# First MLP of a two-layer trunk: 14 of the 16 pairs of up blocks by a Strassen scheme with seven products

## The chip, the cores and the metric

The kernel runs on one core of a Trainium2 chip, in one launch. The metric is the device time of that launch in microseconds (us); lower is better. Engines are called as the profile calls them: PE is TensorE's matmul, PEld its weight load, DVE is VectorE, ACT is ScalarE, POOL is GpSimd, SP is SyncE, which here issues DMAs.

## The reference

512 tokens of width 1024 pass two layers. Layer 0 mixes by an attention over chosen keys, layer 1 by a gated depthwise convolution; each is followed by an MLP of width 4096 with a squared ReLU. Cut to what matters:

```python
def reference(x, ...):
    h = x                                    # 1 x 512 x 1024, fp32
    for i in range(2):
        hn = rmsnorm(h, norm_mix_g[i])
        h = h + (dsa_mixer if i == 0 else conv_mixer)(hn, ...)
        h = h + sq_relu_mlp(rmsnorm(h, norm_mlp_g[i]), mlp_w1[i], mlp_w2[i])
    return rmsnorm(h, final_g)
# sq_relu_mlp(x, w1, w2) = square(relu(x @ w1)) @ w2, w1 1024 x 4096, w2 4096 x 1024
```

The change touches the MLP of layer 0, and what stands at its two ends.

## The kernel before

Activations lie transposed, 128 features by 512 tokens a tile; `hT[c]` (c = 0 to 7) is the residual. An fp32 product is made of three matmuls with operands of type fp32r: high part by high part, high by low, low by high (`mm3`, L91 to L93). `scaled` makes the two parts of the activations, `ghi[c]` on ACT (L174) and `glo[c]` on DVE (L175). `split` makes those of a piece of weights, 128 rows by 4 x 128: `whi` on ACT (L86), `wlo` on DVE (L87). Such a piece is called a unit here; it feeds 12 matmuls. Weights come in loads of 1 MB (L76, on SP's queue, two buffers `wraw`): one load is two blocks of 128 output columns, four units. Split units wait in the pool `wsplit_mid` (12 buffers of each part).

The MLP runs in four groups of 1024 hidden features. A group has 8 up blocks (`up_proj`: 24 matmuls of 512 columns each into a PSUM bank; then `hr` on DVE, which is ReLU and the norm's scale, `hf` and `hh`, two squares on ACT, and `hl` on DVE, the low part of the square) and 8 down blocks of 24 matmuls (`proj` on the hidden tiles; DVE adds each to `hT[c]`). The norm's factor `rmsb` isn't ready when the first MLP starts, so block 0 runs before it. All engines take their instructions in the order that the tile framework's scheduler wrote down; only the last down projection has PE's order by hand, since there the norm of the next mixer and the first products of its projection (`pw1_first`) are woven in. `stacked_taps` makes the diagonal matrices of the convolution on POOL (33 operations, L700) after group 0.

Of the kernel before, what the change touches and what calls it, by code (L numbers as in the profile page):

```python
# [18 lines left out]
P = 128  # L19
# [21 lines left out]

WHOLE = 5

ROW = 512
FILL = 64


@with_exitstack
def kernel(
# [24 lines left out]
    def load(w, k0, kn, c0, cn):  # L74
        t = wraw.tile([P, kn, cn], F32, tag="wraw", name="wraw")
        nc.sync.dma_start(t, rows(w)[:, k0:k0 + kn, c0:c0 + cn])  # L76
        return t

    wsplit = []

    def split(src, eng=None, pool=None, tag="w", bufs=None):

        a, b = src.shape[1], src.shape[2]
        hi, lo = ((pool or wsplit[-1]).tile([P, whole(a * b)], F32R, tag=tag + x, name=tag + x, bufs=bufs)
                  [:, :a * b].rearrange("p (a b) -> p a b", a=a) for x in ("hi", "lo"))
# [50 lines left out]
        return block  # L136


    fill = small.tile([P, FILL // 4], F32, name="fill")
    nc.gpsimd.memset(fill, 0.0)  # L140
    ident = const.tile([P, P], F32, name="ident")
    make_identity(nc, ident)
    ones = const.tile([P, P], F32, name="ones")
# [73 lines left out]


    w_in = dsa_w_in[0]
    with tc.tile_pool(name="wsplit_att", bufs=5) as ws, \  # L220
            tc.tile_pool(name="att", bufs=1) as att, \
            tc.tile_pool(name="att_ps", bufs=2, space=PSUM) as att_ps:

        wsplit.append(ws)

        def lg():
            return att_ps.tile([P, S], F32, tag="lg", name="lg")
# [398 lines left out]
                    wo_end(c, oproj([c])[0])  # L626


    def up_proj(w, rr, pool, st=None, block=None, ahead=()):

        block = block or proj(w, g2)
        hid = []

        def hidden(ps):
            r = pool.tile([P, S], F32, tag="hr", name="hr", bufs=2)
            nc.vector.scalar_tensor_tensor(r, ps, 0.0, rr[0], op0=OP.max, op1=OP.mult)  # L636
            f = pool.tile([P, S], F32, tag="hf", name="hf", bufs=2)
            nc.scalar.activation(f, r, AF.Square)
            th = pool.tile([P, S], F32R, tag="hh", name="hh", bufs=10)
            tl = pool.tile([P, S], F32R, tag="hl", name="hl", bufs=10)  # L640
            nc.scalar.activation(th, r, AF.Square)  # L641
            nc.vector.tensor_sub(tl, f, th.bitcast(F32))  # L642
            hid.append((th, tl))

        done = 0
        if st is not None:
            first = list(ahead) or block([0])
            cols = rms_cols(st)
            first += block([1]) if len(first) < 2 else []
            rr[:] = [broadcast(cols, NB, bank("bc"))]  # L650
            for ps in first:
                hidden(ps)
            done = 2
        for j in range(done, KC):
            hidden(block([j])[0])
        return hid

# [4 lines left out]
    def pw1_first(k):  # L662

        for i, p in enumerate((aproj, gproj)):
# [7 lines left out]
    conv_ctx = ExitStack()
    late = conv_ctx.enter_context(tc.tile_pool(name="late", bufs=1))
    diags = [late.tile([P, max(TAPS0[c][0], TAPS1.get(c, (0, 0))[0]), 4, 32], F32, name=f"diag{c}")
             for c in range(KC)]

    def stacked_taps(pool):

        cw4 = pool.tile([P, 2 * P], F32, name="cw4")
        sel = pool.tile([P, 32], F32, name="sel")
        nc.gpsimd.tensor_add(sel, ident[:, 0:32], ident[:, 32:64])
        for z in (2, 3):
            nc.gpsimd.tensor_add(sel, sel, ident[:, z * 32:(z + 1) * 32])
        ps = bank("cw4_ps")
        for i in range(2):
            r = pool.tile([P, 4, 32], F32, name=f"cwr{i}")
            if i:
                nc.gpsimd.memset(r, 0.0)  # L690
            for a in range(4 - i):
                t = 16 * i + 4 * a
                nc.sync.dma_start(r[a * 32:(a + 1) * 32],
                                  conv_w_dw[0][t:t + 4].rearrange("s (g i) -> g s i", i=32))
            nc.tensor.transpose(ps[:, i * P:(i + 1) * P], r.rearrange("p s i -> p (s i)"), ident)
        nc.vector.tensor_copy(cw4, ps[:, :2 * P])
        for c in range(KC):
            for a in range(diags[c].shape[1]):
                k0 = a * 32 + 4 * c
                nc.gpsimd.tensor_mul(diags[c][:, a], sel.unsqueeze(1).to_broadcast([P, 4, 32]),  # L700
                                     cw4[:, k0:k0 + 4].unsqueeze(2).to_broadcast([P, 4, 32]))

    with tc.tile_pool(name="mlp", bufs=1) as mlp:
        rr = []
        for g in range(NG - 1):
            hid = up_proj(mlp_w1[0][:, g * D:(g + 1) * D], rr, mlp, st if g == 0 else None)
            down = proj(mlp_w2[0][g * D:(g + 1) * D, :], hid)
            for c in range(KC):
                nc.vector.tensor_add(hT[c], down([c])[0], hT[c])
            if g == 0:  # L710
                stacked_taps(mlp)
        hid = up_proj(mlp_w1[0][:, DFF - D:], rr, mlp)
        down = proj(mlp_w2[0][DFF - D:, :], hid)
        st = rms_start()
        with tc.manual_schedule(engines={PE}):
            for c in range(KC):
                nc.vector.tensor_add(hT[c], down([c])[0], hT[c])
                scaled(c, vec("mix", KC + c))
                rms_add(st, c)
                if c:  # L720
                    pw1_first(c - 1)
            aps = aproj([1], kept=pw1_kept[0], ks=range(4), last=False)
            pw1_first(KC - 1)
            ps = bank("rms_ps")
            cols = rms_cols(st, ps)
            aproj([1], kept=pw1_kept[0], pss=aps, ks=range(4, KC), first=False)
            rr = [broadcast(cols, NB, ps)]
            table(AF.Sigmoid, ghi[KC - 1].bitcast(F32))


    HS = S // 2
    halves = [slice(0, HS), slice(HS, S)]
    with tc.tile_pool(name="cv", bufs=1) as cv, \
            tc.tile_pool(name="dram", bufs=1, space=bass.MemoryType.DRAM) as dram, \
# [6 lines left out]
        with tc.tile_pool(name="cv_t", bufs=2) as cv_t:  # L741
# [14 lines left out]
            def taps(c, cs, npe, npool):  # L756
# [13 lines left out]
                w = n + 4 * (npe - 1)  # L770
                flat = dram.tile([P, w + 3], F32, name=f"flat{c}_{cs.start}")
                nc.sync.dma_start(flat, sh(0, w + 3 - n))
                sh4 = cv_t.tile([P, 4, S + 4 * (TAPS // 4 - 1)], F32, tag="sh4", name="sh4")
                for z in range(4):
                    nc.sync.dma_start(sh4[z * 32:(z + 1) * 32, :, :w],
                                      flat.rearrange("(j i) x -> i j x", j=4)[:, :, z:z + w])
# [166 lines left out]
    with tc.tile_pool(name="m2", bufs=1) as m2, \  # L943
# [95 lines left out]
```

## Time and profile before

| | |
|---|---|
| time, median of 3 runs | 1187.97 us (1187.29 to 1189.49) |
| the profiled execution | 1186.75 us, span 1185.0 us (1.75 us lie around the span) |
| PE, PEld busy | 1150.8 us (97%), 948.5 us (80%) |
| DVE, ACT, POOL busy | 663.3 us (56%), 498.2 us (42%), 247.5 us (21%) |
| the first MLP | about 281 to 645 us |

Busy times of PE overlap, since its matmuls are pipelined, so spacing is read from the starts of successive matmuls. In a row of a timeline the numbers in square brackets are the idle time of the engine ahead of it, and what released it; a row with xN is N instructions without a gap. A window row gives, for a stretch, each engine's busy time with its count, then TensorE's granted clock as a share of full speed, the share of the DMA engines and GB/s.

### The profile page before, as it was taken

What the parts mean: (1) busy time and instruction counts of PE and PEld (TensorE: products, weight loads), DVE (VectorE), ACT (ScalarE), POOL (GpSimd) and SP (SyncE); (2) the same over time, 40 slices, a digit from 0 to 9 for tenths busy, and PEclk for the clock granted to TensorE, in tenths of its full rate; (3) what the DMA queues carried; (4) which work ended last, traced back from release to release, by engine and by line L of the source; (5) the groups of instructions that cost most, each with busy time, mean ns of one, the idle gap of its engine ahead of it and who ended that gap; (6) DMA issues with size and microseconds to landing.
All of it is one profiled execution on the core that took longest, in us unless ns stands there. A gap on an engine that the chain in (4) does not pass through costs nothing.

```text
span 1185.0 us, 15284 instructions
## 1 busy us (share of the span) xinstructions
PE 1150.8 (97%) x5828; PEld 948.5 (80%) x5828; DVE 663.3 (56%) x1195; ACT 498.2 (42%) x936; POOL 247.5 (21%) x248
## 2 busy tenths in 40 slices
PE   7999999999999999999999988899999999999997
PEld 6778888877888888888888666689888888888886
DVE  4589854476434434434444998878544434434434
ACT  5353454545423423423435544466632432432422
POOL 2436643322005000000012667632100000000000
PEclk8999999999999999999999998999999999999999
DMA  6122222215233323322323563533322332332211
GB/s 229 36 71 72 89 84 77 71 36 182 78 100 107 98 80 107 107 83 78 125 71 116 151 172 91 161 108 115 117 86 92 107 107 72 106 107 92 86 36 71
DMA packets 104353, 117.84 MB, mean 99 GB/s; under 512 B 3817, under 2 KB 87609, under 8 KB 104280
## 3 DMA queue, kind: packets, MB, share of 16 engines
q1 hardware_dynamic: 102440, 112.89, 30.6%
q10 hardware_dynamic: 1840, 3.97, 0.9%
q8 instruction: 46, 0.75, 0.3%
q14 instruction: 27, 0.22, 0.1%
HBM read 112.56 MB, written 4.29 MB: 99 GB/s over the span
## 4 chain that ended last, share of the span: by engine, by line
PE 81%; DVE 12%; DMA 2%; issue 2%; ACT 1%; POOL 1%; SPq 0%; POOLq 0%; DVEq 0%; ACTq 0%
PE mm L91 19%; PE mm L93 19%; PE mm L92 19%; PE dps L93 5%; PE dps L92 5%; PE dps L91 5%; DVE score L482 2%; DVE m L480 2%; DVE conv L802 2%; DVE wlo L87 2%; DVE pa L798 1%; PE vps L91 1%; PE vps L92 1%; PE vps L93 1%; DMA xs<-in_x_dram 1%
## 5 line engine op out<-in xcount | busy, mean ns | idle before, releaser
L86 ACT ACTIVATE whi<-wraw 128x512 fp32r<-128x512 f32 x378 | 234.6, 631 | 469.9 <-PE mm L92 317.1
L92 PE MATMUL mm<-glo,whi 128*128 128x512 f32 (+1 forms) x928 | 337.0, 365 | 1.2 <-DVE glo L175 1.2
L93 PE MATMUL mm<-ghi,wlo 128*128 128x512 f32 (+1 forms) x928 | 337.1, 365 | 0.0
L91 PE MATMUL mm<-ghi,whi 128*128 128x512 f32 (+1 forms) x928 | 334.6, 366 | 1.9 <-ACT whi L86 0.8
L87 DVE TENSOR_TENSOR wlo<-wraw,whi 128x512 fp32r<-128x512 f32 x325 | 233.5, 726 | 177.7 <-ACT whi L86 174.1
L92 PEld LDWEIGHTS mm<-glo,whi 128*128 128x128 f32 x928 | 175.0, 189 | 31.0 <-issue 2.4
L91 PEld LDWEIGHTS mm<-ghi,whi 128*128 128x128 f32 x928 | 173.1, 189 | 32.6 <-issue 2.8
L93 PEld LDWEIGHTS mm<-ghi,wlo 128*128 128x128 f32 x928 | 175.0, 189 | 28.7 <-issue 1.1
L93 PE MATMUL mm<-hh,wlo 128*128 128x512 f32 x256 | 99.6, 389 | 0.0
L92 PE MATMUL mm<-hl,whi 128*128 128x512 f32 x256 | 99.6, 389 | 0.0
L92 PE MATMUL dps<-wlo,hh 128*128 128x512 f32 x256 | 99.6, 389 | 0.0
L91 PE MATMUL mm<-hh,whi 128*128 128x512 f32 x256 | 99.1, 389 | 0.0
L91 PE MATMUL dps<-whi,hh 128*128 128x512 f32 x256 | 99.1, 389 | 0.0
L93 PE MATMUL dps<-whi,hl 128*128 128x512 f32 x256 | 98.6, 389 | 0.0
L636 DVE SCALAR_TENSOR_TENSOR hr<-mm,rmsb 128x512 f32<-128x512 f32 x64 | 44.1, 691 | 91.9 <-PE mm L93 90.2
L87 POOL TENSOR_TENSOR wlo<-wraw,whi 128x512 fp32r<-128x512 f32 x53 | 70.9, 1342 | 89.6 <-ACT whi L86 89.5
L183 POOL TENSOR_TENSOR fr<-v,mhalf 128x1 f32<-128x1 f32 x4 | 2.2, 548 | 340.2 <-DVE v L181 340.2
L642 DVE TENSOR_TENSOR hl<-hf,hh 128x512 fp32r<-128x512 f32 x64 | 44.6, 697 | 41.9 <-ACT hh L641 41.9
L206 POOL TENSOR_TENSOR ss<-sq 128x512 f32<-128x512 f32 (+1 forms) x4 | 5.7, 1434 | 270.3 <-ACT sq L201 270.3
L790 POOL TENSOR_TENSOR pa<-pa,pt 128x512 f32<-128x512 f32 (+1 forms) x43 | 53.6, 1249 | 32.6 <-ACT pt L788 30.5
L92 PEld LDWEIGHTS mm<-hl,whi 128*128 128x128 f32 x256 | 48.0, 188 | 10.1
L92 PEld LDWEIGHTS dps<-wlo,hh 128*128 128x128 f32 x256 | 48.0, 188 | 10.0
(257 smaller groups left out, 1588.2 us busy)
## 6 DMA issues: line engine op xcount, KB each, us to landing
wraw<-in_mlp_w_dram SPq DMA_DIRECT2D x64, 1024.0 KB, 5.2
wraw<-in_conv_w_pw_dram SPq DMA_DIRECT2D x12, 1024.0 KB
wraw<-in_dsa_w_in_dram SPq DMA_DIRECT2D x10, 1024.0 KB, 9.1
wraw<-in_dsa_w_out_dram SPq DMA_DIRECT2D x4, 1024.0 KB, 4.9
sh<-flat SPq DMA_DIRECT2D x12, 260.0 KB, 3.6
sh<-flat SPq DMA_DIRECT2D x20, 138.0 KB, 2.8
xw<-in_dsa_w_in_dram ACTq DMA_DIRECT2D x4, 584.0 KB, 7.4
xs<-in_x_dram SPq DMA_DIRECT2D x4, 512.0 KB, 12.1
```

The lines of the kernel that those rows point to most:

```text
L86: nc.scalar.activation(hi, src, AF.Copy)
L87: (eng or nc.vector).tensor_sub(lo, src, hi.bitcast(F32))
L91: nc.tensor.matmul(ps, wh, xh, start=start, stop=False)
L92: nc.tensor.matmul(ps, wh, xl, start=False, stop=False)
L93: nc.tensor.matmul(ps, wl, xh, start=False, stop=stop)
L480: nc.vector.max(m8s[-1], score[i])
L482: nc.vector.match_replace(score[i], m8s[i - 1], score[i], TAKEN)
L636: nc.vector.scalar_tensor_tensor(r, ps, 0.0, rr[0], op0=OP.max, op1=OP.mult)
L642: nc.vector.tensor_sub(tl, f, th.bitcast(F32))
L790: nc.gpsimd.tensor_add(pa, pa, pt)
L798: nc.vector.scalar_tensor_tensor(pa, sh(t), wt(t), pa, op0=OP.mult, op1=OP.add)
L802: nc.vector.scalar_tensor_tensor(cps, sh(t), wt(t), cps, op0=OP.mult, op1=OP.add)
```

## The change

The weights of two up blocks (256 hidden features by 1024 inputs) are seen as a 2 x 2 matrix of pieces a11 to a22, and the activations as a 2 x 2 matrix whose pieces are 512 inputs by 256 tokens. A Strassen scheme in Winograd's form makes such a product with seven products of pieces instead of eight, of 12 matmuls with 256 columns each. Sums of weight pieces (`cs`, s1 to s4) are made on DVE for each pair, differences of activations once, and the products are put together by copies on ACT and adds on DVE.

The first four up blocks stay plain. Behind them `differences` and `settle` make the operands: e2, e3, e4 (high and low part, in new tiles), and d1, which is written over the second half of `ghi[i]` and `glo[i]`, i = 0 to 3. The other 28 blocks run as 7 calls of `two_pairs`. After the first call, half a down projection (4 blocks) and a call of `two_pairs` take turns; the last group's down projection stands as before. PE's order in the whole MLP is now the order of the code.

The pool of split weights has 8 buffers in this MLP; `wsplit_mid` with 12 opens behind it. `stacked_taps` comes just ahead of the last down projection, since its tiles share room with the operands. Instructions which set unused bytes are moved too.

```diff
@@ up_proj: how many blocks, and how many buffers of hidden tiles, are arguments now
-    def up_proj(w, rr, pool, st=None, block=None, ahead=()):
+    def up_proj(w, rr, pool, st=None, block=None, ahead=(), n=KC, bufs=10):
...
-    wsplit.append(ctx.enter_context(tc.tile_pool(name="wsplit_mid", bufs=12)))
+    m1_ctx = ExitStack()
+    wsplit_pool(m1_ctx, "wsplit_m1", 8, 32 + ROW - SHIFT)
...
-        for g in range(NG - 1):
-            hid = up_proj(mlp_w1[0][:, g * D:(g + 1) * D], rr, mlp, st if g == 0 else None)
-            down = proj(mlp_w2[0][g * D:(g + 1) * D, :], hid)
-            for c in range(KC):
-                nc.vector.tensor_add(hT[c], down([c])[0], hT[c])
-            if g == 0:
-                stacked_taps(mlp)
-        hid = up_proj(mlp_w1[0][:, DFF - D:], rr, mlp)
-        down = proj(mlp_w2[0][DFF - D:, :], hid)
...
+        def first_rows(i):
+            x = tmp.tile([P, S], F32, tag="sq", name="x1")
+            nc.scalar.activation(x, hT[i], AF.Copy, scale=vec("mlp", i))
+            nc.vector.tensor_sub(x[:, t1], x[:, t1], x[:, t2])
+            return x[:, t1], x[:, t2]
+
+        def differences(i):
+            c = i + 4
+            d1, x12 = first_rows(i)
+            x2 = mlp.tile([P, S], F32, tag="ua", name="x2", bufs=2)
+            nc.scalar.activation(x2, hT[c], AF.Copy, scale=vec("mlp", c))
...
+            nc.vector.tensor_add(v[:, 0], d1, x2[:, t2])
+            nc.vector.tensor_sub(v[:, 1], x12, x2[:, t2])
+            nc.vector.tensor_sub(v4, x2[:, t1], v[:, 0])
+            hi, lo = triple(2 * i), triple(2 * i + 1)
+            for src, at in ((v, slice(0, 2)), (v4.unsqueeze(1), slice(2, 3))):
+                nc.scalar.activation(hi[:, at], src, AF.Copy, scale=-1.0)
+                nc.vector.scalar_tensor_tensor(lo[:, at], src, -1.0, hi[:, at].bitcast(F32),
+                                               op0=OP.mult, op1=OP.subtract)
...
+        def settle(i):
+            c = i + 4
+            d1, _ = first_rows(i)
+            nc.scalar.activation(ghi[i][:, t2], d1, AF.Copy)
+            nc.vector.tensor_sub(glo[i][:, t2], d1, ghi[i][:, t2].bitcast(F32))
...
+        PRODUCTS = {"p1": ("a11", "b11"), "p2": ("a12", "b21"), "q5": ("s1", "d1"), "q6": ("s2", "e2"),
+                    "p7": ("s3", "e3"), "p3": ("s4", "b22"), "p4": ("a22", "e4")}
+        def pair(w, p):
+            raw = load(w, 0, KC, 2 * p * P, 2 * P)
...
+            def plain(name):
+                of = {"s1": ("a21", "a22"), "s2": ("s1", "a11"), "s3": ("a21", "a11"), "s4": ("s2", "a12")}
...
+                    a[name] = mlp.tile([P, 4, P], F32, tag="cs", name="cs", bufs=5)
+                    nc.vector.tensor_add(a[name], x, y)
...
+            def product(ps, name, start):
...
+                hi, lo = split(plain(wn))
+                for k in range(4):
+                    xh, xl = xop[xn, k]
+                    for n, (l, r) in enumerate(((hi, xh), (hi, xl), (lo, xh))):
+                        nc.tensor.matmul(ps, l[:, k, :], r, start=start and k == n == 0, stop=k == 3 and n == 2,
...
+        def two_pairs(w, p, hid):
...
+            for z in range(2):
+                al[z] = bank("al")[:, t1]
+                prods[z](al[z], "p1", True)
+            for z in range(2):
...
+                prods[z](ga[z], "q5", True)
...
+                nc.scalar.activation(ua[z][:, t1], al[z], AF.Copy)
+            for z in range(2):
+                prods[z](al[z], "q6", False)
...
+                nc.scalar.activation(ub[z][:, t2], ga[z], AF.Copy)
+            for z in range(2):
...
+                prods[z](be[z], "p2", True)
+                nc.scalar.activation(ua[z][:, t2], al[z], AF.Copy)
+                nc.vector.tensor_add(ua[z][:, t1], be[z], ua[z][:, t1])
+            for z in range(2):
+                prods[z](al[z], "p7", False)
+                nc.vector.tensor_add(ub[z][:, t2], al[z], ub[z][:, t2])
+            for z in range(2):
+                prods[z](ga[z], "p3", False)
+                nc.vector.tensor_add(ua[z][:, t2], ga[z], ua[z][:, t2])
+                nc.vector.scalar_tensor_tensor(ua[z], ua[z], 0.0, rr[0], op0=OP.max, op1=OP.mult)
+                squares(2 * z, ua[z])
+            for z in range(2):
+                prods[z](al[z], "p4", False)
+                scaled_min(ub[z], ub[z][:, t2], t2)
+                scaled_min(ub[z], al[z], t1)
+                squares(2 * z + 1, ub[z])
...
+            hid = up_proj(w1[0], rr, mlp, st, n=4, bufs=NH)
+            for i in range(4):
+                differences(i)
+            for i in range(4):
+                settle(i)
+            two_pairs(w1[0], 2, hid)
+            for g in range(NG):
+                down = proj(mlp_w2[0][g * D:(g + 1) * D, :], hid)
+                if g < NG - 1:
+                    hid = []
+                    downs(down, range(4))
+                    two_pairs(w1[g + 1], 0, hid)
+                    downs(down, range(4, KC))
+                    two_pairs(w1[g + 1], 2, hid)
+        stacked_taps()
...
+    m1_ctx.close()
+    wsplit_pool(ctx, "wsplit_mid", 12, 32)
```

The first place is DVE's order around the fourth plain block. Before, a block brought `hr`, `hl` and two `wlo`:

```order
L636 SCALAR_TENSOR_TENSOR hr<-mm,rmsb 128x512
L87 TENSOR_TENSOR wlo<-wraw,whi 128x512
L642 TENSOR_TENSOR hl<-hf,hh 128x512
L87 TENSOR_TENSOR wlo<-wraw,whi 128x512
L636 SCALAR_TENSOR_TENSOR hr<-mm,rmsb 128x512
```

Now 33 instructions follow the `hr` of the fourth plain block (L648) up to the last part of d1; these are the last twelve of them (x is a scaled copy of the residual, e a difference or its low part, `glo_110` to `glo_113` are the low parts of d1 for i = 0 to 3):

```order
L758 TENSOR_TENSOR e_3069<-x_3064,x_3067 128x256
L745 TENSOR_TENSOR x_3083<-x_3083 128x256
L763 SCALAR_TENSOR_TENSOR e_2821<-e_3055,e_3059 128x256
L773 TENSOR_TENSOR glo_110<-x_3078,ghi_102 128x256
L759 TENSOR_TENSOR e_3070<-x_3067,e_3069 128x256
L763 SCALAR_TENSOR_TENSOR e_2823<-e_3069,e_2822 128x512
L745 TENSOR_TENSOR x_3088<-x_3088 128x256
L773 TENSOR_TENSOR glo_111<-x_3083,ghi_103 128x256
L745 TENSOR_TENSOR x_3093<-x_3093 128x256
L763 SCALAR_TENSOR_TENSOR e_2823<-e_3070,e_2822 128x256
L773 TENSOR_TENSOR glo_112<-x_3088,ghi_104 128x256
L773 TENSOR_TENSOR glo_113<-x_3093,ghi_105 128x256
```

So the parts of d1, which the first call's second product reads, come last, behind the operands e that later products read.

The second place is DVE's order at the end of a call of `two_pairs` that a first half of a down projection follows (here in group 1; the same at the end of groups 0 and 2). The `wlo` are those of the down projection's first blocks, `hr<-al`, `ua` and `hl` make the hidden tiles, `cs` is a sum for the next pair:

```order
L852 SCALAR_TENSOR_TENSOR ua<-ua,rmsb 128x512
L101 TENSOR_TENSOR wlo<-wraw,whi 128x512
L827 SCALAR_TENSOR_TENSOR hr<-al,rmsb 128x256
L822 TENSOR_TENSOR hl<-hf,hh 128x512
L101 TENSOR_TENSOR wlo<-wraw,whi 128x512
L794 TENSOR_TENSOR cs<-wraw 128x512
L822 TENSOR_TENSOR hl<-hf,hh 128x512
L101 TENSOR_TENSOR wlo<-wraw,whi 128x512
L822 TENSOR_TENSOR hl<-hf,hh 128x512 x2
```

The four `hl`, which the down blocks read, come behind the splits for the first two pairs of those blocks and a sum for the next pair; the two `hl` of the hidden tiles `hr` are last.

The third place is ACT's order at the end of the MLP, where the convolution's norm factor `rmsb` is made. Before:

```order
L86 ACTIVATE whi<-wraw 128x512 x3
L98 ACT_TABLE_LOAD
L98 ACTIVATE table<-ghi_111 128x1
L86 ACTIVATE whi<-wraw 128x512
L193 ACTIVATE rmsb<-rms_ps 128x512
```

Now:

```order
L186 ACTIVATE ghi_109<-hT_101,pm_91 128x512
L213 ACTIVATE sq<-hT_101 128x512
L112 ACT_TABLE_LOAD
L112 ACTIVATE table<-ghi_109 128x1
L100 ACTIVATE whi<-wraw 128x512 x6
L205 ACTIVATE rmsb<-rms_ps 128x512
```

Six splits, into the newly opened pool, stand ahead of `rmsb` where one stood.

## Rows read from the trace of the kernel before

**Rows 1.** The page: span, busy times, PE in 40 slices, its granted clock.

```profile
span 1185.0 us, 15284 instructions
...
PE 1150.8 (97%) x5828; PEld 948.5 (80%) x5828; DVE 663.3 (56%) x1195; ACT 498.2 (42%) x936; POOL 247.5 (21%) x248
...
PE   7999999999999999999999988899999999999997
...
PEclk8999999999999999999999998999999999999999
```

**Rows 2.** Windows of 20 us, in the first MLP and in 256-column products.

```profile
400.00:420.00 20.00, 20.00 (x90) 16.57 (x89) 8.64 (x14) 7.29 (x13) 0.00 (x0) 1.00 0.33 106
800.00:820.00 20.00, 20.00 (x169) 19.93 (x168) 16.15 (x40) 13.35 (x28) 2.98 (x2) 1.00 0.22 71
```

**Rows 3.** PE's timeline (start, duration): first and last of 54 steps, 512 columns.

```profile
399.64 0.39 PE L93 MATMUL mm<-ghi,wlo 128*128 128x512 f32 x1
...
411.88 0.39 PE L93 MATMUL mm<-hh,wlo 128*128 128x512 f32 x1
```

**Rows 4.** PE's timeline: first and last of 68 steps of 256 columns.

```profile
803.74 0.28 PE L92 MATMUL mm<-glo,whi 128*128 128x256 f32 x1
...
811.90 0.28 PE L91 MATMUL pw<-ghi,whi 128*128 128x256 f32 x1
```

**Rows 5.** DVE's timeline at the start of the first MLP.

```profile
283.10 0.16 DVE L181 TENSOR_SCALAR v<-rms_ps 128x4 f32<-128x4 f32 x1 [1.61 <-PE rms_ps L215]
...
284.87 0.88 DVE L190 TENSOR_SCALAR diag<-ident,rms 128x128 f32<-128x128 f32 x4 [0.31 <-POOL rms L183]
285.66 3.10 DVE L87 TENSOR_TENSOR wlo<-wraw,whi 128x512 fp32r<-128x512 f32 x5
...
300.52 0.69 DVE L636 SCALAR_TENSOR_TENSOR hr<-mm,rmsb 128x512 f32<-128x512 f32 x1 [1.59 <-PE mm L93]
```

**Rows 6.** DVE's timeline beside 256-column work.

```profile
804.54 0.42 DVE L862 TENSOR_TENSOR glo<-u,ghi 128x256 fp32r<-128x256 f32 x1
804.88 0.42 DVE L856 TENSOR_TENSOR u<-u,dr 128x256 f32<-128x256 f32 x1
```

**Rows 7.** Groups by line and shape: busy us, mean ns | idle ahead.

```profile
L92 PE MATMUL mm<-hl,whi 128*128 128x512 f32 x256 | 99.6, 389 | 0.0
...
L175 DVE SCALAR_TENSOR_TENSOR glo<-hT,pm,ghi 128x512 fp32r<-128x512 f32 x8 | 6.0, 751 | 1.4 <-ACT ghi L174 1.4
...
L900 DVE SCALAR_TENSOR_TENSOR hT<-mm,pv,hT 128x256 f32<-128x256 f32 x12 | 5.5, 479 | 6.2 <-PE mm L93 6.2
```

**Rows 8.** ACT's timeline: four splits without a gap.

```profile
282.60 2.20 ACT L86 ACTIVATE whi<-wraw 128x512 fp32r<-128x512 f32 x4 [3.01 <-DMA wraw<-in_mlp_w_dram]
```

**Rows 9.** Windows around PE's idle time in the convolution.

```profile
719.00:720.00 1.00, 0.84 (x5) 0.25 (x9) 0.96 (x2) 0.83 (x2) 1.00 (x2) 0.50 0.00 0
...
724.00:725.00 1.00, 1.00 (x8) 0.22 (x4) 0.00 (x0) 0.51 (x1) 1.00 (x3) 0.52 0.00 0
```

**Rows 10.** PE's timeline there.

```profile
719.15 5.35 PE L780 MATMUL conv<-sh,diag 128*32 128x512 f32 x24 [4.83 <-DVE conv L802]
```

**Rows 11.** The page, DMA issues: KB each, us from issue to landing.

```profile
wraw<-in_mlp_w_dram SPq DMA_DIRECT2D x64, 1024.0 KB, 5.2
```

**Rows 12.** Timeline of the end of the first MLP.

```profile
644.24 0.63 ACT L86 ACTIVATE whi<-wraw 128x512 fp32r<-128x512 f32 x1 [1.53 <-PE mm L92]
...
645.35 0.60 ACT L193 ACTIVATE rmsb<-rms_ps 128x512 f32<-128x512 f32 x1 [0.49 <-PE rms_ps L191]
...
646.00 0.50 PE L91 MATMUL mm<-ghi,whi 128*128 128x512 f32 x1 [0.69 <-ACT rmsb L193]
```

**Rows 13.** Groups of POOL: the diagonal matrices of the convolution.

```profile
L700 POOL TENSOR_TENSOR diag<-sel,cw 128x128 f32<-128x128 f32 x33 | 15.3, 502 | 82.1 <-DVE cw L696 82.1
```

**Rows 14.** Timeline of a DVE instruction beside a POOL one.

```profile
617.32 1.33 POOL L209 TENSOR_TENSOR ss<-ss,sq 128x512 f32<-128x512 f32 x1 [5.76 <-ACT sq L201]
...
617.73 1.47 DVE L87 TENSOR_TENSOR wlo<-wraw,whi 128x512 fp32r<-128x512 f32 x1 [0.22 <-ACT whi L86]
```

More of the change, by code (lines that the diff above doesn't have):

```diff
@@ L44 @@
 ROW = 512
-FILL = 64
+SHIFT = 64
+HS = S // 2
+NH = 12
+LATE = ((5,), (6,), (7,), (0, 2), (1, 4), (3,))
 @with_exitstack
@@ L79, with wsplit_pool @@
     wsplit = []
+    def wsplit_pool(stack, name, bufs, fill):
+        pool = stack.enter_context(tc.tile_pool(name=name, bufs=bufs, side="right"))
+        for part in ("whi", "wlo"):
+            nc.gpsimd.memset(pool.tile([P, S], F32R, tag=part, name=part).bitcast(F32), 0.0)
+        nc.gpsimd.memset(pool.tile([P, fill // 4], F32, tag="fill", name="fill", bufs=1), 0.0)
+        wsplit.append(pool)
     def split(src, eng=None, pool=None, tag="w", bufs=None):
@@ L136, in proj @@
         return block
-    fill = small.tile([P, FILL // 4], F32, name="fill")
-    nc.gpsimd.memset(fill, 0.0)
     ident = const.tile([P, P], F32, name="ident")
@@ L219 @@
     w_in = dsa_w_in[0]
-    with tc.tile_pool(name="wsplit_att", bufs=5) as ws, \
+    with ExitStack() as ws, \
             tc.tile_pool(name="att", bufs=1) as att, \
             tc.tile_pool(name="att_ps", bufs=2, space=PSUM) as att_ps:
-        wsplit.append(ws)
+        wsplit_pool(ws, "wsplit_att", 5, 32)
         def lg():
@@ L638, in hidden @@
             nc.scalar.activation(f, r, AF.Square)
-            th = pool.tile([P, S], F32R, tag="hh", name="hh", bufs=10)
-            tl = pool.tile([P, S], F32R, tag="hl", name="hl", bufs=10)
+            th = pool.tile([P, S], F32R, tag="hh", name="hh", bufs=bufs)
+            tl = pool.tile([P, S], F32R, tag="hl", name="hl", bufs=bufs)
             nc.scalar.activation(th, r, AF.Square)
@@ L653, in up_proj @@
             done = 2
-        for j in range(done, KC):
+        for j in range(done, n):
             hidden(block([j])[0])
@@ L669, in pw1_first, with stacked_taps @@
                 pw1.extend(ps)
-    wsplit.append(ctx.enter_context(tc.tile_pool(name="wsplit_mid", bufs=12)))
+    m1_ctx = ExitStack()
+    wsplit_pool(m1_ctx, "wsplit_m1", 8, 32 + ROW - SHIFT)
     conv_ctx = ExitStack()
     late = conv_ctx.enter_context(tc.tile_pool(name="late", bufs=1))
[L674 to L682, printed above, removed]
+    diags = {}
+    def stacked_taps():
+        for i, cc in enumerate(LATE):
+            ns = [max(TAPS0[c][0], TAPS1.get(c, (0, 0))[0]) for c in cc]
+            t = late.tile([P, sum(ns), 4, 32], F32, tag=f"late{i}", name=f"diag{i}")
+            for c, n in zip(cc, ns):
+                diags[c] = t[:, :n]
+                t = t[:, n:]
+        t = tmp.tile([P, S], F32, tag="sq", name="cw4")
+        cw4, sel = t[:, :2 * P], t[:, 2 * P:2 * P + 32]
         nc.gpsimd.tensor_add(sel, ident[:, 0:32], ident[:, 32:64])
@@ L687, in stacked_taps @@
         for i in range(2):
-            r = pool.tile([P, 4, 32], F32, name=f"cwr{i}")
+            r = tmp.tile([P, S], F32, tag="sq", name="cwr")[:, :P].rearrange("p (s i) -> p s i", s=4)
             if i:
@@ L772, in taps @@
                 nc.sync.dma_start(flat, sh(0, w + 3 - n))
-                sh4 = cv_t.tile([P, 4, S + 4 * (TAPS // 4 - 1)], F32, tag="sh4", name="sh4")
+                sh4 = cv_t.tile([P, 4, S + 12], F32, tag="sh4", name="sh4")
                 for z in range(4):
```

50 lines of the change are left out of this document (48 added, 2 removed).

## Prediction

> **What bounds the kernel now.** I read the page first, for which engine is busy all the time: PE is at 97%, its slices are nearly all nines, DVE is at 56% [rows 1]. Then windows inside the first MLP: PE is busy in all of 20 us at full granted clock, while DVE works 8.64 and ACT 7.29 us of it [rows 2]. So this stage is bound by PE's own spacing, and the two other engines have room on average. The groups by line show why no block ends late: the matmuls that read `hl` never waited (0.0 us idle ahead of 256 of them) [rows 7]. What the change takes from PE counts in full, as long as DVE and ACT still deliver in time at each place; averages can't say that, so I follow their orders.
>
> **PE's saving.** Matmuls of 512 columns: 54 steps from 399.64 to 411.88, 12.24/54 = 0.2267 us each [rows 3]. With 256 columns: 68 steps from 803.74 to 811.90, 8.16/68 = 0.1200 us [rows 4]. A pair was 48 x 0.2267 = 10.88 us and is 84 x 0.1200 = 10.08: 0.80 us less, 14 times: **-11.2 us**. The seven eighths of the scheme thus become only 0.93, as a fixed part stays with each half-width matmul. At 256 columns PEld is busy 19.93 of 20 us and PE still keeps the pace [rows 2], so I take no further loss.
>
> The Trainium skill ("TensorE: Matmul & The Clock Gate", section "Back-to-back issue gap") gives columns/2.4 plus 2.5 ns for an isolated gap at full clock, by which a pair would save 1.18 us and the change 16.5; the rows above have 226.7 and 120.0 ns, not 215.7 and 109.2, so the measured step decides.
>
> **Prices on the other engines.** Where instructions follow at once, each starts about 0.08 us before the last one's end. DVE: 128x512 subtractions, five in 3.10 us, 0.60 each [rows 5]; 256 wide, 804.54 to 804.88, 0.34 [rows 6]; scalar_tensor_tensor 0.751 and 0.479 alone, so 0.66 and 0.40 in a row [rows 7]. ACT: four splits in 2.20, 0.55 [rows 8]. A call of `two_pairs` holds 168 x 0.12 = 20.16 us of PE. DVE: 8 sums, 14 `wlo` and 4 `hl` (26 x 0.60), 6 adds (0.34), 2 and 4 scalar_tensor_tensor (0.66, 0.40): 20.6 us. Half a down projection is 96 x 0.2267 = 21.8 us of PE beside 12 x 0.60 = 7.2 of DVE. Together 27.8 of 41.9: enough on average, but inside a call DVE has no slack at all.
>
> **First call of two_pairs.** Before, `v` and the diagonals hold DVE until about 285.7, and the fourth block's `hr` starts at 300.52, when PE has finished that block [rows 5]. Until then DVE now has 16 instructions of 0.60, 3 of 0.66, 3 of 0.34, or 12.6 us, from about 286.9, when the second pair's load has landed behind the first one's: done at 299.5, then it waits for PE, as that `hr` did before. Behind it stand 33 instructions up to the last part of d1: 21 of 256 columns (7.14 us), 4 of 512 (2.40), 4 scalar_tensor_tensor of 512 (2.64), 4 of 256 (1.60): 13.8 us. With `hr` from 300.55 to 301.2 this ends at **315.0**. PE ends both p1 at 300.45 + 2 x 1.44 = 303.3 and wants the last d1 at 303.3 + 10 x 0.12 = 304.5. It waits **10.5 us**. Queued behind on DVE are the `wlo` of q6; they have the two q5 to be made in. If the e operands, made ahead of d1, cost nothing (12 adds and 8 scalar_tensor_tensor, 8.3 us), 2.2 would be left: the lower bound. ACT has about as much to do there, in alternation with DVE; if each waited for the other at a third of the steps, some 4 us come on top: the upper bound 14.5. I take 10.5.
>
> **Clock.** In the convolution PE idled 4.83 us [rows 10], and the granted clock was 0.50 (1.2 GHz) until 724 to 725 us [rows 9], so 5.4 us of work ran at half speed, a loss of 2.7. Here PE idles some 8 us before the first d1 arrives, but half of what follows waits anyway: **+1.5** (0 to 2.7).
>
> **End of a call ahead of a first half down, four times.** Count from the call's start. The down weights need a `wraw` buffer. The first pair's is read last by the split for its p4, the 13th product; with 8 split buffers that waits for the fifth product's, at 5 x 1.44 = 7.2, and with the split made it is about 8.7. The load then needs 5.2 us [rows 11] and lands at 13.9; its first `whi` and `wlo` end at 15.25. From there to the first `hl` of a tile `hr` DVE's order holds 20 instructions without a gap (12 x 0.60, 3 x 0.34, 2 x 0.66, 3 x 0.40), 10.7 us: 26.0. PE ends the call at 20.16, makes the down block's first unit (2.72) and one step more (0.68), and wants that `hl` with the second matmul of the next: 23.8. **2.2 us, four times: +8.8.** If the load landed in 3 us, nothing; if ACT's squares, which stand behind a split that waits for a buffer, are late too, 3.5 each: 0 to 14. In the second half of a down projection all eight tiles are old, and nothing waits.
>
> **The rest.** At the end six splits of 0.55 stand on ACT ahead of `rmsb`, where one stood, and the first waits for the last unit to free a buffer as the one at 644.24 did [rows 12]: `rmsb` 2.5 us later, PE's restart at 646.00 too. The splits must be made anyway, so part is given back: **+1** (0 to 2.5). The diagonals (15.3 us of POOL) [rows 13] are covered by 43.5 us of the last down projection; they can stretch a DVE instruction from 0.69 to 1.47 [rows 14], at most 2 us there. At the start two more copies on ACT: **+0.4** (0 to 1.2).
>
> **Sum** on the profiled execution: 1186.75 - 11.2 + 10.5 + 1.5 + 8.8 + 1.0 + 0.4 = 1197.75. The median lies 1.2 above that execution: **1199 us**.
>
> **Rivals.**
> (a) Faster: DVE keeps up. The place is the end of the four calls and the d1 chain; it decides if the load lands by 11.7 on the call's clock, so that DVE's run begins 2.2 us earlier, and if the chain's e part is made in DVE's gaps before 300.5. For it: DVE at 43% of a window now [rows 2]; against it: both orders put `hl` and d1 last. With all stalls of the calls gone and 2.2 to 5 left at d1: 1188 - 11.2 + 5 = about 1182 (1177 to 1185).
> (b) The gain is cancelled, no more: one of the two kinds of wait stays away. Without those of the calls: 1199 - 8.8 = 1190; with half of the first call's too, 1185 to 1190.
> (c) Worse: ACT and DVE wait in turn, each wait at its upper bound: +4 at d1, +5 over the calls, about 1207.
> (d) By the shorter steps of 1.18 us a pair the stalls grow by what PE is sooner at each wait; only where nothing waits is it gained: 1199 - 5.3 = 1194 at most. The Trainium skill's gap (above) is this rival; both steps in the trace speak against it.
> That the products aren't made is excluded: PE's order shows 84 matmuls of 256 columns for a pair.
>
> **Chances.** Forecast (1191 to 1203) 0.43; (a) 0.27; (b) 0.12; (c) 0.15; (d) 0.03. The range takes in most of (a) and (c): 1178 to 1207. What this kernel's measurement can tell from no change is 0.2%, 2.4 us. Faster: (a) and a little of (b), 0.29. Same: 0.09. Slower: the forecast, (c), (d) and the rest of (b), 0.62.
>
> **What would show it.** Right: PE's starts 0.120 us apart within a call; PE idle of about 10 us before the first call's q5, released by DVE's d1 (L773), and granted clock 0.50 behind it; four idle times of about 2 us in the first down block, released by `hl` (L822). Wrong: the load of the down weights lands before 12 on a call's clock, or the d1 chain ends near 304, as when DVE's sums are made far ahead; or steps at 256 columns with different weights each 12 matmuls are not 0.120.

## The result, and the profile after

The changed kernel takes 1219.03 us (median of 4 runs, 1217.0 to 1220.06), beside 1188.73 us of the kernel before in the same rounds: a ratio of 1.0252, interval 1.0232 to 1.0272. It is slower, as forecast, by 30 us in place of 11, and lies outside the stated range. The profiled execution took 1220.06 us, its span 1218.3 (33.3 more than before).

The page of the kernel after, to be held against [rows 1]:

```profile
span 1218.3 us, 16617 instructions
...
PE 1150.5 (94%) x6332; PEld 968.8 (80%) x6332; DVE 751.2 (62%) x1381; ACT 538.7 (44%) x1044; POOL 253.5 (21%) x257
...
PE   7999999999799999999999898699999999999997
...
PEclk9999999999899999999999999889999999999999
```

PE's row has a new gap in its eleventh slice, at the start of the first MLP, and a deeper one in the convolution (slice 26, 6 where the row before had 8). The granted clock dips in slice 11 and in slices 26 and 27. To see how much each part of the program lost, I read `rmsb`, which is made once at the start of each stage. Before, and then after (the last two numbers of a row are the first and last start; `bc` stands for both MLPs, `rms_ps` for the convolution):

```profile
L193 ACT ACTIVATE rmsb<-bc x2: 599/599/599, 290.0 to 843.3; 128x512 f32<-128x512 f32 x2
...
L193 ACT ACTIVATE rmsb<-rms_ps x1: 598/598/598, 645.4 to 645.4; 128x512 f32<-128x512 f32 x1
```

```profile
L205 ACT ACTIVATE rmsb<-bc x2: 599/601/603, 291.4 to 876.6; 128x512 f32<-128x512 f32 x2
...
L205 ACT ACTIVATE rmsb<-rms_ps x1: 577/577/577, 665.9 to 665.9; 128x512 f32<-128x512 f32 x1
```

From marker to marker the first MLP took 355.4 and takes 374.5 us (+19.1), the convolution 197.9 and 210.7 (+12.8), the rest 341.7 both times; 1.4 were lost ahead of it all (from profile to profile this first start lies between 290.0 and 291.4, at 291.3 in e11, which has none of the change, so the change need not be the cause). What PE waited for inside the MLP (line waited for: us in total, times, longest):

```profile
PE mm L106 <- DVE hl L822: 8.7, 6, 2.2
PE ga L803 <- ACT ghi L772: 6.4, 1, 6.4
PE ga L803 <- DVE glo L773: 1.7, 2, 1.3
PE mm L105 <- ACT hh L821: 1.4, 1, 1.4
```

These are the two kinds of wait of the forecast, d1 (L772, L773) and the hidden tiles (L821, L822), 18.2 us together. PE's timeline shows how a stall extends beyond its wait: the rows are the start of the first call, the wait for d1, the start of the first half down projection behind that call, its wait for `hl`, and where it ends; then a later call and a second half without a wait, and the wait for `hl` behind the call that follows.

```profile
302.36 0.28 PE L803 MATMUL al<-ghi,whi 128*128 128x256 f32 x1
...
311.70 0.58 PE L803 MATMUL ga<-ghi,whi 128*128 128x256 f32 x1 [6.36 <-ACT ghi L772]
...
334.30 0.40 PE L105 MATMUL mm<-hh,whi 128*128 128x512 f32 x1
...
340.62 0.59 PE L106 MATMUL mm<-hl,whi 128*128 128x512 f32 x1 [2.05 <-DVE hl L822]
...
360.46 0.28 PE L803 MATMUL al<-ghi,whi 128*128 128x256 f32 x1
...
380.25 0.39 PE L105 MATMUL mm<-hh,whi 128*128 128x512 f32 x1
...
402.01 0.28 PE L803 MATMUL al<-ghi,whi 128*128 128x256 f32 x1
...
428.25 0.50 PE L106 MATMUL mm<-hl,whi 128*128 128x512 f32 x1 [2.22 <-DVE hl L822]
```

A call without a wait takes 380.25 - 360.46 = 19.79 us, a half down projection without one 402.01 - 380.25 = 21.76. The first call takes 334.30 - 302.36 = 31.94, 12.15 more; the half behind it 360.46 - 334.30 = 26.16, 4.40 more, though its waits are only 2.2. The granted clock tells most of the rest: 0.50 (1.2 GHz) behind both waits, until about 320.4 and 344.3. It does not fall behind every such wait: in group 2 PE waited for `hl` 0.88 and 2.05 us, up to 516.47, and the clock behind that stayed at 1.00 (the last row).

```profile
316.00:318.00 2.00, 2.00 (x9) 1.83 (x9) 0.45 (x2) 0.57 (x2) 1.21 (x4) 0.50 0.11 16
...
320.00:322.00 2.00, 2.00 (x17) 2.00 (x17) 0.69 (x1) 1.23 (x3) 0.00 (x0) 0.90 0.05 8
...
341.00:343.00 2.00, 2.00 (x6) 1.61 (x5) 0.16 (x1) 0.00 (x0) 0.00 (x0) 0.50 0.92 322
...
344.00:345.00 1.00, 1.00 (x5) 0.88 (x4) 1.00 (x3) 0.43 (x1) 0.00 (x0) 0.86 0.00 0
...
518.00:520.00 2.00, 2.00 (x10) 1.66 (x9) 0.41 (x1) 0.35 (x1) 0.00 (x0) 1.00 0.30 104
```

In the first half of the convolution DVE is the engine that is always busy, 9.86 us or more of each 10 from 676 to 786, while PE has gaps:

```profile
736.00:746.00 10.00, 6.54 (x57) 2.92 (x50) 9.86 (x15) 4.43 (x8) 9.92 (x9) 1.00 0.77 184
...
766.00:776.00 10.00, 6.56 (x95) 3.96 (x93) 10.00 (x13) 6.30 (x14) 9.10 (x9) 1.00 0.95 273
```

Groups of DVE by line, before and after, from one `rmsb` to the next:

```profile
L87 DVE TENSOR_TENSOR wlo<-wraw,whi 128x512 fp32r<-128x512 f32 x57 | 47.1, 846 | 7.8 <-ACT whi L86 7.5
L798 DVE SCALAR_TENSOR_TENSOR pa<-u,cw,pa 128x256 f32<-128x256 f32 (+1 forms) x34 | 27.7, 814 | 0.9 <-POOL pa L793 0.6
```

```profile
L101 DVE TENSOR_TENSOR wlo<-wraw,whi 128x512 fp32r<-128x512 f32 x65 | 53.6, 848 | 13.8 <-ACT whi L100 12.9 <-PE mm L106 0.7
L968 DVE SCALAR_TENSOR_TENSOR pa<-u,cw,pa 128x256 f32<-128x256 f32 (+1 forms) x34 | 33.3, 987 | 0.2
```

Eight more splits of weights fall into the stage (+6.5 us of DVE), and 34 operations of the convolution are stretched (+5.6): 28 of them, in place of 19, run for most of their time beside an operation of POOL, as the one in [rows 14] did. ACT shows why at the boundary, against [rows 12]:

```profile
662.73 3.23 ACT L100 ACTIVATE whi<-wraw 128x512 fp32r<-128x512 f32 x6 [5.81 <-PE mm L107]
665.86 0.58 ACT L205 ACTIVATE rmsb<-rms_ps 128x512 f32<-128x512 f32 x1
```

The six splits wait for PE's last matmul of the MLP, since only then the pool of 12 takes over the room of the pool of 8; before, weights could be split ahead there. No other `whi` starts between 639.54 and 662.73; before, eight start from 625.60 on:

```profile
L86 ACT ACTIVATE whi<-wraw x8: 631/634/635, 625.6 to 644.2; 128x512 fp32r<-128x512 f32 x8
```

### The profile page after: what moved, and what is told of

It reads as the page before. It is cut to its first block, busy times and chain, and to the rows that moved or that the text cites. A ratio compares the mean times of both kernels' runs of the same rounds, so it can differ in the third digit from the quotient of the medians.

```text
span 1218.3 us, 16617 instructions
## 1 busy us (share of the span) xinstructions
PE 1150.5 (94%) x6332; PEld 968.8 (80%) x6332; DVE 751.2 (62%) x1381; ACT 538.7 (44%) x1044; POOL 253.5 (21%) x257
## 5 line engine op out<-in xcount | busy, mean ns | idle before, releaser
L105 PE MATMUL mm<-ghi,whi 128*128 128x512 f32 (+1 forms) x704 | 250.8, 360 | 5.0 <-ACT rmsb L205 2.9
L106 PE MATMUL mm<-glo,whi 128*128 128x512 f32 (+1 forms) x704 | 251.5, 358 | 0.5 <-DVE glo L187 0.4
L107 PE MATMUL mm<-ghi,wlo 128*128 128x512 f32 (+1 forms) x704 | 251.4, 358 | 0.0
L105 PEld LDWEIGHTS mm<-ghi,whi 128*128 128x128 f32 x704 | 133.0, 191 | 25.5 <-ACT rmsb L205 3.1
L106 PEld LDWEIGHTS mm<-glo,whi 128*128 128x128 f32 x704 | 133.6, 190 | 21.4 <-issue 1.7
L107 PEld LDWEIGHTS mm<-ghi,wlo 128*128 128x128 f32 x704 | 133.7, 190 | 20.7 <-issue 1.7
L718 POOL TENSOR_TENSOR diag<-cw 128x128 f32<-128x128 f32 x33 | 17.2, 557 | 280.9 <-DVE cw L714 280.9
L100 ACT ACTIVATE whi<-cs 128x512 fp32r<-128x512 f32 x56 | 35.3, 630 | 58.4 <-PE mm L106 37.6
L803 PE MATMUL al<-e,whi 128*128 128x256 f32 x336 | 60.5, 282 | 0.0
L105 PEld LDWEIGHTS mm<-hh,whi 128*128 128x128 f32 x256 | 49.2, 192 | 12.1 <-ACT hh L821 1.8
```

The costliest lines, as they stand in the source:

```text
L105: nc.tensor.matmul(ps, wh, xh, start=start, stop=False)
L106: nc.tensor.matmul(ps, wh, xl, start=False, stop=False)
L107: nc.tensor.matmul(ps, wl, xh, start=False, stop=stop)
L803: nc.tensor.matmul(ps, l[:, k, :], r, start=start and k == n == 0, stop=k == 3 and n == 2, skip_group_check=not start)
```

## The experiments

Each time is a median; ratios are to the kernel before in the same rounds. Stages are read from the rows of `rmsb` as above: MLP, convolution, rest. They belong to the one profiled execution, which can lie off the median, most of all in e2 (1197.81 us), e6 (1204.94) and e7 (1202.75).

**e1_order.** d1 ahead of the e operands, and another order of products.

```diff
-            for i in range(4):
-                differences(i)
             for i in range(4):
                 settle(i)
+            for i in range(4):
+                differences(i)
@@ two_pairs; allocations, copies and adds move with their products
             for z in range(2):
                 prods[z](al[z], "p1", True)
+            for z in range(2):
+                prods[z](be[z], "p2", True)
             for z in range(2):
                 prods[z](ga[z], "q5", True)
+            for z in range(2):
+                prods[z](ga[z], "p3", False)
             for z in range(2):
                 prods[z](al[z], "q6", False)
-            for z in range(2):
-                prods[z](be[z], "p2", True)
             for z in range(2):
                 prods[z](al[z], "p7", False)
-            for z in range(2):
-                prods[z](ga[z], "p3", False)
```

> The changed kernel with two edits: d1 is made ahead of the e operands, and a call takes its products as p1, p2, q5, p3, q6, p7, p4, so that eight products that read no e come first. Theory A (the first call's stall is DVE's chain of differences, and the half clock behind it): the 9.4 us that PE waited there for ACT's and DVE's parts shrink to under 3, and most of the spell of half clock of 10 us goes; about 10 to 13 us less than the changed kernel, near 1207. Rival (PE waits there for the second pair's weights or for PSUM, and the order of the operands doesn't matter): the same 1219 within 2.

1206.88 us, 1.0156 (1.0137 to 1.0175); 363.3, 209.9, 341.7. The total came as theory A said, but not by its mechanism: PE's waits are

```profile
PE ga L803 <- ACT hr L842: 5.4, 1, 5.4
PE al L803 <- ACT ua L847: 3.9, 5, 1.1
...
PE mm L106 <- DVE hl L822: 0.8, 3, 0.3
```

The first call still waits, now for ACT's copy of q5, which is queued behind the same chain; it got 5.2 us shorter (26.74). The other calls got longer, 20.8 to 21.5, as q6 and p7 now follow each other with one product between, too few for ACT's copy. What was won lies where I hadn't looked: with p3 early, the tiles `ua` are finished sooner, and `hl` is no longer late: the three first halves take 22.1 to 22.4 in place of 25.3 to 26.4.

**e2_down_twos.** The first two down blocks of a group as one.

```diff
-            for c in cc:
-                nc.vector.tensor_add(hT[c], down([c])[0], hT[c])
+            first = dict(zip(cc[:2], down(cc[:2]))) if cc[0] == 0 else {}
+            for c in cc:
+                nc.vector.tensor_add(hT[c], first[c] if c in first else down([c])[0], hT[c])
```

> The changed kernel with one edit: the first two down blocks of each group run as one, all k of the old hidden tiles for both first. PE then comes to the new hidden tiles 2.7 us later. Theory A (the waits for hl are short lateness of DVE, 2.2 us each, and each calls a spell of half clock of 3.4 us that costs 1.7): waits for hl and hh fall from 10.1 to under 2, three or four half-clock spells go; 12 to 16 us less than the changed kernel, about 1204. Rival (DVE is behind for good and the wait only moves to another instruction): under 4 us less.

1202.42 us, 1.0121 (1.009 to 1.0153); 359.9, 204.0, 341.7. No wait for `hl` or `hh` is left, and the halves take 21.76 each. The MLP is 14.6 us shorter, while the waits removed were 10.1 and 2.5 of new ones came at the last down projection; three spells of half clock of 3.4 us went as well, which is 5.1. The wait for d1 stays.

```profile
PE ga L803 <- ACT ghi L772: 6.4, 1, 6.4
PE ga L803 <- DVE glo L773: 1.7, 2, 1.3
PE mm L106 <- DVE glo L187: 1.4, 1, 1.4
PE mm L105 <- ACT ghi L186: 1.1, 1, 1.1
```

Theory A holds here. That the convolution also fell by 6.7 was not expected (`pa` 30.6 us there in place of 33.3); the scheduler writes the order of that stage anew with every edit, and what in it made the difference was not tried.

**e3_plain, e4_plain12, e5_plain12_448.** No Strassen products at all, for the rest of the change by itself.

```diff
@@ e3: no differences, no settle; four plain blocks for each call
-                    two_pairs(w1[g + 1], 0, hid)
+                    two_plain(w1[g + 1], 0, hid)
@@ e4: e3 and one pool
-    wsplit_pool(m1_ctx, "wsplit_m1", 8, 32 + ROW - SHIFT)
+    wsplit_pool(ctx, "wsplit_m1", 12, 32 + ROW - SHIFT)
...
-    m1_ctx.close()
-    wsplit_pool(ctx, "wsplit_mid", 12, 32)
@@ e5: e4 with all tiles at one offset within 512 bytes
-    wsplit_pool(ctx, "wsplit_m1", 12, 32 + ROW - SHIFT)
+    wsplit_pool(ctx, "wsplit_m1", 12, 32)
-        mlp_fill = mlp.tile([P, SHIFT // 4], F32, name="mlp_fill")
-        nc.gpsimd.memset(mlp_fill, 0.0)
```

> The changed kernel with plain up blocks in place of all Strassen products (no differences, no sums); pools of split weights (8, then 12 opened behind the MLP), taps ahead of the last down projection, turns of half a down projection with four up blocks stay. Theory B (the convolution stage is 13 us longer because fewer weights are split ahead of it): the stage from one rmsb to the next stays near 211 us as in the changed kernel, the MLP itself is as before, the total 10 to 15 above the kernel before, about 1201. Rival (the longer convolution comes from the Strassen part, by what it leaves late at the boundary): the stage returns to 198, the total to 1188 to 1191.

1203.08 us, 1.0129 (1.0114 to 1.0144); 363.4, 208.6, 341.7. The longer convolution is there without Strassen: theory B. But the MLP is 8 us longer too, with no wait in it before `rmsb`.

> The run before it, with one pool of 12 split buffers through the MLP and the convolution in place of 8 and then 12. Theory B: the six splits ahead of rmsb go, eight more wlo are made before the convolution, and the stage is back at about 198 us; total about 1188. Rival (the taps on POOL right ahead of the last down projection, or the order of the scheduler, cost it): the stage stays above 205.

1202.05 us, 1.0118 (1.0103 to 1.0133); 361.2, 199.1, 349.7. The convolution went back, as theory B said, and the total did not: the second MLP, which the edit doesn't touch, took 8 us more. PE never waited in it. So its matmuls themselves were slower. In windows of the first MLP (e4, then e5) 20 us hold fewer of them:

```profile
390.00:410.00 20.00, 20.00 (x87) 16.06 (x86) 9.28 (x15) 8.04 (x14) 0.00 (x0) 1.00 0.34 106
```

```profile
390.00:410.00 20.00, 20.00 (x90) 16.57 (x89) 8.72 (x13) 7.89 (x13) 0.00 (x0) 1.00 0.33 106
```

The built programs' addresses gave theory C. In the kernel before the tiles of these products start at a multiple of 512 bytes; after the change split weights and hidden tiles of the first MLP do, and `ghi`, `glo` lie at 448 within 512. In e4 the one pool of weights stays at a multiple of 512 in the second MLP too, whose other tiles all lie at 448.

> The run with plain blocks and one pool of 12, with one edit: the 480 unused bytes of the split pool and the 64 of the MLP pool go, so that split weights, hidden tiles and activations all start at the same offset within 512 bytes (448), as all of them did in the kernel before (0). Theory C (a 512-column matmul steps at 0.2267 us where weights and moving tiles have the same offset within 512 bytes, and at about 0.234 where they differ): the up blocks of the first MLP and the whole second MLP return to 0.2267, the total falls from 1202 to 1188 to 1190. Rival (the steps are slower since the tiles lie at other addresses altogether, or by the order on the other engines): no change, 1202.

1189.41 us, 1.0007 (0.9998 to 1.0016); 355.8, 199.4, 341.7. Theory C holds: this is the kernel before again.

**e6_order_twos.** The first two edits together.

> The changed kernel with both edits of the first two runs (d1 first and the new order of products; first two down blocks as one). Theory A: their gains add, since they are at different places: 1219 - 12 - 16 = about 1190. Rival (both lived on the same half-clock spells or on a shift of the convolution's order, which is drawn anew each time): 1196 to 1200.

1211.01 us (its four runs lie from 1204.94 to 1218.36), 1.0191 (1.0148 to 1.0234); the profiled one 1204.94 with 364.5, 205.9, 341.6. It fits neither range; the two gains don't add, and both edits together are no faster than either alone. By the waits both had won at the same place, the late `hl`. The new order's waits for ACT stay (4.8 and 4.1 us), and the calls take up to 21.8.

**e7_early12.** The pool of 12 from the last down projection on.

```diff
+        stp = st_ctx.enter_context(tc.tile_pool(name="stp", bufs=1))   # e5 to e7, cs, ua
...
+        st_ctx.close()
+        m1_ctx.close()
+        wsplit_pool(ctx, "wsplit_mid", 12, 32)
         stacked_taps()
```

> The changed kernel with other pools only: operands e5 to e7, sums and ua in a pool of their own that closes with the last call; the pool of 12 split buffers opens there, ahead of the last down projection, not behind it; all tiles at one offset within 512 bytes. Theory B (the convolution is longer because few weights are split ahead of it): the stage from rmsb to rmsb falls from 211 to 198 to 200, the wait for rmsb of 2.9 to under 1; total about 1206. Rival (the order alone is unlucky): the stage stays above 205.

1207.38 us, 1.0149 (1.0128 to 1.0169); 368.2, 200.2, 341.7. Theory B: 57 splits in the stage again, and PE waits for `rmsb` 0.7, as before the change. Two of its first halves have waits for `hl` of 2.04 and 2.05 us with the granted clock at 1.00 all through: they take 24.12 and 24.21, which is 2.3 and 2.4 over a half without a wait (21.79). The third, with a wait of 2.94 and 0.50 behind it, takes 26.65.

**e8_all.** All edits so far.

> All edits together: d1 first, products p1, p2, q5, p3, q6, p7, p4, first two down blocks as one, 12 split buffers from the last down projection on, one offset. If theories A, B and C hold and add, what is left of the change is its saving on PE, 11 to 14, less 5 to 8 of waits in the first call: 1180 to 1184, faster than before. Rival (DVE, full within each call, makes a new wait elsewhere): 1188 or more.

1204.38 us, 1.0127 (1.011 to 1.0144); 371.1, 199.3, 341.7. The rival, in a place nobody named: the last down projection waits for `ghi`, and the order of products has its waits again.

```profile
PE mm L105 <- ACT ghi L186: 6.0, 1, 6.0
PE ga L803 <- ACT hr L842: 5.2, 1, 5.2
PE al L803 <- ACT ua L847: 4.0, 5, 1.5
```

ACT's queue there holds eight splits that wait for loads ahead of the first `ghi` of the next mixer; that two down blocks as one put them there was not tried by itself.

**e9_group0_plain, e10_group0_plain_8.** The original order of products; all of group 0 plain (12 pairs by Strassen), so that the operands are made beside 22 us more of plain work; two blocks as one in groups 0 to 2 only. e9 with the early pool of 12 and one offset, e10 with the pools of the change.

```diff
-            hid = up_proj(w1[0], rr, mlp, st, n=4, bufs=NH)
+            hid = up_proj(w1[0], rr, mlp, st, bufs=NH)
...
-            two_pairs(w1[0], 2, hid)
```

> The changed kernel with: all eight up blocks of the first group plain (12 of 16 pairs by Strassen), the operands made beside the end of that group and its first half down; the first two down blocks of groups 0 to 2 as one; the pool of 12 split buffers opened ahead of the last down projection; one offset within 512 bytes. If the loss is what theories A (DVE's chain ahead of the first call, hl late at each first half down, half clock behind both), B (few weights split ahead of the convolution) and C (offsets) say, and nothing else: the first MLP is 355.4 - 12 x 0.98 = 343.6 plus 2 to 4 of waits at the last down projection, the convolution 199.5 as in the runs with 12 buffers, total 1178 to 1182: faster than before by 0.5 to 0.8%. Rival (Strassen's calls are bound by DVE, and every edit moves the wait): the first MLP stays over 352, the total at 1188 or more.

1183.14 us, 0.9952 (0.994 to 0.9965): faster than both kernels, by 0.5% of the kernel before, and just above the range. 349.1, 198.5, 341.7; no wait for d1, and in the MLP behind group 0

```profile
PE mm L105 <- ACT whi L100: 1.0, 1, 1.0
PE mm L107 <- DVE wlo L101: 0.5, 1, 0.5
PE mm L106 <- DVE glo L187: 0.3, 1, 0.3
```

The calls take 20.15 in place of 19.79, so a pair saves 0.80 and not 0.98; the last run explains that.

> The run before it with the pools of the changed kernel (8 split buffers through the MLP, 12 opened behind it). Theory B: the first MLP as in the run before it, but the wait for rmsb is 2.9 again and the convolution 204 to 211: 6 to 14 above that run. Rival (the pool matters only beside late hl): the same as that run within 3.

1195.92 us, 1.0065 (1.005 to 1.0081); 355.8, 204.6, 341.7. The pool of 8 costs 12.8 here: 6.1 in the convolution, 6.7 up to `rmsb`, where `hl` and `hh` are late at the last down projection (2.4 and 1.3) and the six splits stand again. Of the 6.7, 2.2 are the wait for `rmsb` that theory B has; the rest neither theory had.

**e11_before_offset, e12_offset_448.** Theory C alone, on the kernel before and on the changed one.

```diff
@@ e11
-    fill = small.tile([P, FILL // 4], F32, name="fill")
+    fill = ctx.enter_context(tc.tile_pool(name="gap", bufs=1)).tile([P, FILL // 4], F32, name="fill")
     nc.gpsimd.memset(fill, 0.0)
     wsplit.append(ctx.enter_context(tc.tile_pool(name="wsplit_mid", bufs=12)))
@@ e12: the edit of e5, in the changed kernel
```

> The kernel before, with one edit: its 64 unused bytes stand ahead of the split weights and not ahead of the activations, so that ghi and glo start at 448 within 512 bytes, and split weights and hidden tiles at 0 as before. Theory C: products of ghi and glo with 512 columns step at about 0.234 in place of 0.2267 (768 of them in each MLP, 5.8 us in the first as the run with plain blocks showed, so 11 to 12 in both), those of hidden tiles stay; about 1199. If 256-column steps get shorter by such a difference (0.118 in the changed kernel's calls against 0.120 in the convolution before), the convolution gives back about 1. Rival (the steps come from something else in those kernels): 1188.

1198.95 us, 1.0088 (1.0073 to 1.0103); 360.7, 199.1, 346.3. As forecast, by 64 unused bytes at another place; 88 matmuls in the window where [rows 2] has 90:

```profile
400.00:420.00 20.00, 20.00 (x88) 16.29 (x87) 8.17 (x13) 7.25 (x12) 0.00 (x0) 1.00 0.33 106
```

The convolution gave nothing back (+1.2), though its 256-column steps did get shorter, in part by more than expected: 94 steps in 10.65 us, 0.1133 each, against 0.1200 in [rows 4].

```profile
825.00 0.28 PE L92 MATMUL mm<-glo,whi 128*128 128x256 f32 x1
...
835.65 0.28 PE L93 MATMUL pw<-ghi,wlo 128*128 128x256 f32 x1
```

> The changed kernel with one edit: all tiles at one offset within 512 bytes. By theory C the four plain blocks gain 0.7, and the 256-column steps of the calls, 0.1178 where weights and activations differ, go to 0.1200: 14 x 84 x 0.0022 = 2.6 us more; waits and the convolution as in the changed kernel; about 1221, with the convolution's order free to move it by 5 either way. What counts is the step within a call. Rival (0.1178 belongs to the calls themselves): it stays 0.1178.

1220.02 us, 1.0268 (1.0243 to 1.0292); 375.4, 209.6, 341.7. A call, from its first row to the first of the down block behind it:

```profile
360.12 0.28 PE L801 MATMUL al<-ghi,whi 128*128 128x256 f32 x1
...
380.27 0.40 PE L105 MATMUL mm<-hh,whi 128*128 128x512 f32 x1
```

20.15/168 = 0.1199 a step, against 19.79/168 = 0.1178: theory C here too, with the sign turned round.

## Why the prediction was wrong

**PE's saving: right, a little small.** A call replaces four blocks of 5.44 us, 21.76, by 19.79: 2.0 less, seven times, 13.8 in place of 11.2, as the step was 0.1178 and not 0.1200. That it was shorter is luck: with all tiles at one offset it is 0.1199 (e12). The four plain blocks lost 0.6 by their offset.

**First call: the chain right, its parts in part by luck.** DVE's chain, from the start of the fourth `hr` to the end of the last d1, ran from 302.56 to 316.45: 13.9 us where 14.5 was said (13.8 behind an `hr` of 0.65).

```profile
302.56 0.69 DVE L648 SCALAR_TENSOR_TENSOR hr<-mm,rmsb 128x512 f32<-128x512 f32 x1 [0.98 <-PE mm L107]
...
315.68 0.77 DVE L773 TENSOR_TENSOR glo<-x,ghi 128x256 fp32r<-128x256 f32 x2
```

Wait and clock together were to cost 12.0 and cost 12.15. But the waits were 8.1 in place of 10.5, and the clock took the rest, some 4 in place of 1.5; that the two misses cancel is luck.

**First half down: the wait right, its price wrong.** I said that the down weights land at 13.9 on a call's clock, `hl` comes at 26.0 and PE waits 2.2. In group 1 the call starts at 402.01; the first split of those weights, released by the load, starts at 415.96, at 13.95, and PE goes on at 428.25, at 26.2, after 2.22 us.

```profile
415.96 2.20 ACT L100 ACTIVATE whi<-wraw 128x512 fp32r<-128x512 f32 x4 [4.49 <-DMA wraw<-in_mlp_w_dram]
```

But half clock followed the waits in groups 0 and 1 and at the last down projection, each time for about 3.4 us, and I had priced the clock only where PE idles for 8 us. The three halves are 4.4, 4.6 and 3.5 us longer (the third, with 2.9 of waits, kept the full clock). The last down projection, from its first matmul on a hidden tile to its last, took 51.45 (583.47 to 634.92) and takes 56.80 (596.21 to 653.01), with 2.7 of waits and a spell of its own. Together that is 17.9 in place of 8.8.

**The rest: the step that failed most.** "The splits must be made anyway, so part is given back: +1 (0 to 2.5)" was said of the boundary; it is 2.2 up to `rmsb` and 12.8 behind it. I counted the splits ahead of `rmsb`, and not that the pool of 8, of which four hold the first blocks of the projection, makes nothing ready beyond. Those splits fall on DVE where it is busy all the time, in the first half of the convolution: in all seven profiles with 12 buffers in time the stage is 197.9 to 200.2 with 57 `wlo` in it, in all seven with 8 it is 204.0 to 210.7 with 64 or 65. With only the pools changed (e9 and e10, `pa` 28.4 and 28.6 us) the stage grows by 6.1. The rest of the 12.8 goes with the stretch of `pa` beside POOL: within the seven with 8 buffers it is 28.6 to 30.6 us where the stage takes 204.0 to 205.9, and 33.1 to 33.4 where it takes 208.6 to 210.7. What in the order sets that stretch was not tried.

The sum by what was measured: 1.4 - 13.8 + 0.6 + 12.2 + 17.9 + 2.2 + 12.8 = 33.3, the whole difference of the spans. Rival (a) fell as it stands; e9 shows that DVE does keep up once the chain of operands has other work to lie beside and `hl` more lead. Rival (d) had the direction of the shorter step, not its size, and not its cause (e12).

By e11 and e12 the step at full clock hangs on where the operands lie as well as on the columns, 0.2267 or 0.2333 us at 512 columns, 0.1178 or 0.1199 at 256. The Trainium skill ("TensorE: Matmul & The Clock Gate", "Back-to-back issue gap") gives the isolated gap of a warm matmul, one at full clock, by its columns alone. Where the two differ, the measured step decides.

## What to carry to other kernels

An algorithm that takes work from the engine that bounds a kernel hands it to the others in bursts: follow each burst in the order up to the instruction that PE needs first, and give it lead (another block of independent work) before counting the saving. A wait of 2.0 to 2.2 us on TensorE cost 2.3 to 2.4 where the granted clock stayed at 1.00 (e7), and 4.4 to 4.6 where 0.50 followed; what decides between the two isn't shown. A pool that is made smaller in one stage is paid in the next one, where the engine that fills it may be the bound; and after every change of pools, look at the step of untouched matmuls.

## What the runs showed that I had not expected

Without any wait, matmuls step by where their tiles start within 512 bytes. With split weights and moving tiles at the same offset, 512 columns take 0.2267 us; with the moving tile at 448 and the weights at 0, 0.2333, which over a kernel like this one was 10 us for a shift of 64 bytes (e11: 1198.95 against 1188.66), and 8 us in an MLP that wasn't edited (e4). With 256 columns it is the other way round, 0.1199 and 0.1178 (e12), and down to 0.1133 in the convolution of e11; why that is shorter still isn't shown either. Only these two distances were tried, and what lies behind it isn't shown.
